# The order of the matmuls inside each product P times V, in a two-layer hybrid decoder trunk

## The chip, the cores and the metric

The kernel runs on one core of one Trainium2 chip. The metric is the device time of one execution in microseconds; less is better. A core has a matrix engine (TensorE: PE for its matmuls, PEld for its weight loads), a vector engine (DVE), a scalar engine (ACT), GpSimd (POOL), a queue engine (SP) and 16 DMA engines. Matmuls write their results to PSUM, eight banks of 512 fp32 values in each of 128 partitions; ACT and DVE carry them from there to the on-chip memory SBUF.

## The reference, cut to what matters

512 tokens of width 1024 pass two layers. Each layer is an attention part and a squared-ReLU MLP. What matters here are the attention products, which are all a softmax followed by a sum over keys:

```
# layer A, for each of 12 heads (3 groups of 4), two branches with the same form
p_s = masked_softmax(einsum('bgrqd,bgqkd->bgrqk', q_b, k_g) * scale, m_s)
o_s = einsum('bgrqk,bgqkd->bgrqd', p_s, v_g)            # selected blocks
p_w = masked_softmax(einsum('bgrqd,bgkd->bgrqk', q_b, k_b) * scale, m_w)
o_w = einsum('bgrqk,bgkd->bgrqd', p_w, v_b)             # sliding window
return g_b[..., 0:1] * o_c + g_b[..., 1:2] * o_s + g_b[..., 2:3] * o_w
...
# both layers, 4 heads over 256 memory tokens
p = softmax(einsum('bhqd,bhmd->bhqm', q, k) * scale)
o_mem = einsum('bhqm,bhmd->bhqd', p, v)
...
# layer B, 8 head slots, three dilated windows merged by their softmax sums
s = where(valid, einsum('bhqd,bhqkd->bhqk', q_b[:, gi], k_g) * scale, NEG)
outs.append(einsum('bhqk,bhqkd->bhqd', exp(s - lse), v_g))
```

With 512 tokens the window of 512 and the 16 selected blocks both cover every earlier token, so both branches of layer A are causal attention over different keys and values.

## The kernel before

**The order of things.** Layer A's attention comes first, then its MLP, then layer B's attention, then its MLP. Attention work is cut into items. An item has a front (scores, maximum, exponential, scaling) and a back (transposes of P, their evacuation, and, in the last item of a unit, the product P times V). `attend` (line 126) writes front k+1 before back k, and after each of them takes steps from a list of other work (projections, weight splits, output projection). The order in which the program writes instructions is not yet the order on the engine: line 1782 opens the framework's context with `schedule_with_timeline_sim=True`, which orders each engine's instructions by when they are ready on a simulated timeline, and among ready ones by the order of the program. What order came out is read from the trace. On the chip each engine then takes its list in that order.

**One unit of P times V.** V is the stationary operand, 128 keys by 64 columns; the transposed P is the moving one. Two heads share one PSUM bank, taken from the pool `pO` with a single buffer: the first head writes partitions 0 to 63, the second 64 to 127. So a matmul occupies 64 of the array's 128 columns, and the two heads' matmuls use different halves. A matmul on fp32 data is two instructions on PE. There are 24 units:

- **Layer A, `attn_a` lines 1023 to 1061.** For each of 3 groups, 2 pairs of heads (`pr`) and 2 halves of the queries (`half`, 256 queries each), items run over `hp` (which head of the pair) and `ii` (which 128 queries); the unit is written in the last of the four, hp = 1 and ii = 1. Half 0 has 2 blocks of 128 keys, half 1 has 4, in 2 branches `br`, for 2 heads: 8 and 16 matmuls, the last block of each branch over 128 columns, the others over 256. In half 0 both branches of an item are transposed into one bank and evacuated by one instruction; in half 1 each branch has its own (lines 1039 to 1043), branch 0 first. The transposed P lies in tiles of the tag `pt4`, four buffers. After half 1, `cmp_out` (line 955) adds one more matmul to the same bank and splits the sum for the output projection.
- **Memory attention, `mem_items` lines 600 to 620.** 2 pairs of heads in each layer. A head's P is transposed in 2 items (`ih`); the unit has 2 key blocks for 2 heads, 4 matmuls of 512 columns.
- **Layer B, `close0` line 1567 and `close1` line 1581,** one each for 4 pairs of slots. In `close0` 4 key blocks `j` for 2 slots `s`, 8 matmuls (256 columns, the last block 128); item ih = 0 of a slot brings the transposed columns 0 to 383, ih = 1 columns 384 to 895. In `close1` 4 residues `r` for 2 slots, 8 matmuls of 128 columns; ih = 0 brings r = 0 and 1, ih = 1 brings r = 2 and 3. A slot's items come before those of the next slot.

**Evacuation of transposes.** `evT` (line 656) copies a transposed bank to SBUF: in layer A every third time on DVE (line 658), otherwise on ACT (line 660); in layer B always on ACT. Transposes take banks from the pool `pT`, two buffers.

Of the kernel before, what the change touches and what calls it, by code (L numbers as in the profile page):

```python
# [18 lines left out]
NB = 4  # L19
# [145 lines left out]
class K:  # L165
# [412 lines left out]
    def mem_items(self, kf, qm, kk, outs, seg, need):  # L578

        nc = self.nc  # L580

        def front(h, ih):
            Sp = self.ps(self.pS, [P, 2, NMEM])
            for ii in range(2):
                i = ih * 2 + ii
                for hl in (0, 1):
                    nc.tensor.matmul(
                        Sp[:, ii, :], qm[0][h // 2][:, h % 2, i * P : (i + 1) * P], kk[0][hl][:, h, :],
                        start=hl == 0, stop=hl == 1,
                    )  # L590
            p, sm = self.soft(Sp, 2, NMEM)
            c = self.t("cr", [P, 2])
            nc.vector.reciprocal(out=c, in_=sm)
            for ii in range(2):
                self.pscale(p[:, ii, :], c[:, ii : ii + 1])
            return p

        pT = {}

        def back(h, ih, p):  # L600
            if ih == 0:
                pT[h] = self.t("pt4", [P, 2, S])
            pt = self.ps(self.pT, [P, 2, 2, P])
            for kb in range(2):
                for ii in range(2):
                    nc.tensor.transpose(pt[:, kb, ii, :], p[:, ii, kb * P : (kb + 1) * P], self.idf)
            self.evT(pT[h][:, :, ih * 256 : (ih + 1) * 256].rearrange("p k (i q) -> p k i q", q=P), pt)
            if h % 2 == 0 or ih == 0:
                return
            O = self.ps(self.pO, [P, S])  # L610
            for kb in range(2):
                for hp in range(2):
                    hh = h - 1 + hp
                    nc.tensor.matmul(
                        O[hp * 64 : hp * 64 + 64, :], kf[0][kb][1][:, hh * HD : (hh + 1) * HD], pT[hh][:, kb, :],
                        start=kb == 0, stop=kb == 1,
                    )
            oT = self.t("act", [P, 2, S], F32R)
            self.split(oT, O)
            outs.append(oT)  # L620

        return [Item(front, back, (h, ih), seg, need) for h in range(4) for ih in range(2)]

    def hilo(self, ki, src):
# [336 lines left out]
    def attn_a(self, g, ga, gt, cmp, out):  # L961


        nc = self.nc
        st, cs, Os = {}, [], []

        def cfront(i):
            if not cs:
                cs.extend(self.cmp_scores(g, ga[0], cmp, gt))
            return cs[2](i)  # L970

        def cback(i, s):
            cs[3](i, s)
            if i == NB - 1:
                cs.append(True)
                close()

        def close():
            while Os and len(cs) > 4:
                self.cmp_out(*Os.pop(0), *cs[0:2], out)  # L980

        def front(pr, half, hp, ii):
            q4, kk, v = ga
            h = pr * 2 + hp
            q = q4[pr][:, hp, :]
            i = half * 2 + ii
            n = (i + 1) * P
            blk = slice(i * P, (i + 1) * P)
            sm = self.t("su", [P, 2])
            if i <= 1:  # L990
                Sp = self.ps(self.pS, [P, 2, n])
                for hl in (0, 1):
                    nc.tensor.matmul(Sp, q[:, blk], kk[hl][:, :, 0:n], start=hl == 0, stop=False)
                nc.tensor.matmul(Sp[:, :, blk], self.idb, bcast(self.cm, 1, 2), start=False, stop=True)
                Sb = [Sp[:, 0, :], Sp[:, 1, :]]
                nm = self.t("nm", [P, 2])
                nc.vector.tensor_reduce(out=nm, in_=Sp, axis=AX.X, op=ALU.max, negate=True)
                nms = [nm[:, 0:1], nm[:, 1:2]]
                pp = self.t("p2", [P, 2, n])
                p = [pp[:, 0, :], pp[:, 1, :]]  # L1000
            else:
                Sb, nms = [], []
                for br in range(2):
                    Sp = self.ps(self.pS, [P, n])
                    for hl in (0, 1):
                        nc.tensor.matmul(Sp, q[:, blk], kk[hl][:, br, 0:n], start=hl == 0, stop=False)
                    nc.tensor.matmul(Sp[:, blk], self.idb, self.cm, start=False, stop=True)
                    nm = self.t("nm", [P, 1])
                    nc.vector.tensor_reduce(out=nm, in_=Sp, axis=AX.X, op=ALU.max, negate=True)
                    Sb.append(Sp)  # L1010
                    nms.append(nm)
                p = [self.t("p2", [P, n]) for _ in range(2)]
            o = (4 * g + h) * 3 + 1
            for br in range(2):
                nc.scalar.activation(p[br], Sb[br], AF.Exp, bias=nms[br], accum_out=sm[:, br : br + 1])
            c = self.t("cr", [P, 2])
            nc.vector.reciprocal(out=c, in_=sm)
            nc.vector.tensor_tensor(out=c, in0=c, in1=gt[:, i, o : o + 2], op=ALU.mult)  # L1018
            for br in range(2):
                self.pscale(p[br], c[:, br : br + 1])  # L1020
            return p

        def back(pr, half, hp, ii, p):
            v = ga[2]
            i = half * 2 + ii
            if ii == 0:
                if half == 0:
                    t = self.t("pt4", [P, 2, 2, 256])
                    st[hp] = [t[:, 0], t[:, 1], t]
                else:  # L1030
                    st[hp] = [self.t("pt4", [P, 4, 256]) for _ in range(2)]
            if i <= 1:
                pt = self.ps(self.pT, [P, 2, i + 1, P])
                for br in range(2):
                    for j in range(i + 1):
                        nc.tensor.transpose(pt[:, br, j, :], p[br][:, j * P : (j + 1) * P], self.idf)
                self.evT(st[hp][2][:, :, 0 : i + 1, ii * P : (ii + 1) * P], pt)
            else:
                for br in range(2):
                    pt = self.ps(self.pT, [P, i + 1, P])  # L1040
                    for j in range(i + 1):
                        nc.tensor.transpose(pt[:, j, :], p[br][:, j * P : (j + 1) * P], self.idf)
                    self.evT(st[hp][br][:, 0 : i + 1, ii * P : (ii + 1) * P], pt)
            if hp == 0 or ii == 0:
                return
            if half == 0:
                st["O"] = self.ps(self.pO, [P, S])
            O = st["O"]
            q0 = half * 256
            nj = 2 * half + 2  # L1050
            for br in range(2):
                for j in range(nj):
                    o = P if j == nj - 1 else 0
                    for x in range(2):
                        nc.tensor.matmul(  # L1055
                            O[x * 64 : x * 64 + 64, q0 + o : q0 + 256], v[:, j, br, :], st[x][br][:, j, o:256],
                            start=half == 0 and br == 0 and j == 0, stop=False,
                        )
            if half == 1:
                Os.append((O, pr))  # L1060
                close()

        order = [(pr, half, hp, ii) for pr in range(2) for half in range(2) for hp in range(2) for ii in range(2)]
        need = f"g{g}" if g else None
        return (
            [Item(front, back, a, g, need) for a in order],
            [Item(cfront, cback, (i,), g, "cmp") for i in range(NB)],
        )
# [409 lines left out]
    def attn_b(self, sp, q4, kv, oT, side):  # L1478
# [4 lines left out]
        t0, t1 = {}, {}  # L1483
# [83 lines left out]
        def close0():  # L1567
            vn = kv[1]
            O = self.ps(self.pO, [P, S])
            for j in (0, 2, 1, 3):  # L1570
                n = min(2, NB - j) * P
                for s in range(2):
                    nc.tensor.matmul(
                        O[s * 64 : s * 64 + 64, j * P : j * P + n], vn[:, j, s * HD : (s + 1) * HD],
                        t0[s][:, j * 256 : j * 256 + n], start=j == 0, stop=j == NB - 1,
                    )
            a = self.t("raw", [P, S])
            nc.scalar.activation(a.rearrange("p (r u) -> p r u", r=4), self.perm(O), AF.Copy)
# [2 lines left out]
        def close1():  # L1581
            vp = kv[2]
            O = self.ps(self.pO, [P, S])
            for r in range(4):
                for s in range(2):
                    nc.tensor.matmul(
                        O[s * 64 : s * 64 + 64, r * P : (r + 1) * P], vp[:, r, s * HD : (s + 1) * HD], t1[s][:, r, :],
                        start=True, stop=True,
# [198 lines left out]
```

## Time and profile before

| What | Value |
|---|---|
| time, median of 3 runs | 1309.15 us |
| the 3 runs | 1308.75 to 1311.78 us |
| the profiled execution, its own time | 1312.09 us |
| its span, first to last instruction | 1310.1 us |
| granted TensorE clock, mean over the span | 0.993 |
| DVE busy | 989.7 us (76%) |
| ACT busy | 766.2 us (58%) |
| POOL busy | 537.6 us (41%) |
| matmul instructions of P times V: line 1055 / 614 / 1573 / 1586 | 288 / 32 / 64 / 64 |

How to read it: an engine's busy time is the union of its instructions' times. The ends of matmuls are modelled and successive ones overlap a little, so the time that a group of matmuls really takes is best read from its start to the start of the next instruction on PE. A row of the timeline merges neighbours of one line: `213.25 1.73 PE L1055 ... x16` starts 213.25 us into the span, lasts 1.73 us and holds 16 instructions; a bracket at its end gives the engine's idle time before it and what ended that. The chain of waits is followed back from the last instruction, at each step to what released it. Layer A's attention lies between about 60 and 345 us of the span, layer B's between about 760 and 960 us.

### The profile page before, as it was taken

To read this page: it belongs to the slowest core of one execution; us is meant where nothing else is said; L and a number is where in the kernel's file an instruction comes from. 1 tells how busy PE (TensorE), PEld (TensorE's weight loads), DVE (VectorE), ACT (ScalarE), POOL (GpSimd) and SP (SyncE) were. 2 spreads that over 40 slices of the span, in tenths; PEclk is the share of its full clock that TensorE was granted. 3 is DMA by queue.
4 is the path that set the end of the run, shared out by engine and by line. 5 is a ranking of instruction groups with operands and counts; after the bars stand their busy time and mean duration, and the time that the engine had idled before them with its cause. 6 is when DMAs were issued, how large, how long until landed. Compare 5 with 4: busy or idle time off the path is not lost.

```text
span 1310.1 us, 18597 instructions
## 1 busy us (share of the span) xinstructions
PE 1267.1 (97%) x6425; PEld 1018.0 (78%) x6425; DVE 989.7 (76%) x1687; ACT 766.2 (58%) x1763; POOL 537.6 (41%) x569
## 2 busy tenths in 40 slices
PE   8998999999999999999999999999899999999998
PEld 6776677677787888888878898787578788788886
DVE  6878768764669678697799768776658968779678
ACT  5657657673465364554656477776756545355462
POOL 3756375542165142251333946441417424134241
PEclk9999999999999999999999999989999999999999
DMA  8313211023422525415244333012232442633423
GB/s 307 103 59 100 65 33 57 9 66 105 153 97 74 170 81 175 145 65 177 81 141 145 102 104 95 22 32 73 88 122 94 128 145 81 184 106 115 144 96 113
DMA packets 52686, 139.11 MB, mean 106 GB/s; under 512 B 5776, under 2 KB 14992, under 8 KB 52592
## 3 DMA queue, kind: packets, MB, share of 16 engines
q1 hardware_dynamic: 51376, 134.66, 32.4%
q0 software_dynamic: 640, 2.21, 0.5%
q8 instruction: 51, 0.84, 0.3%
q10 hardware_dynamic: 576, 1.05, 0.2%
q14 instruction: 43, 0.35, 0.1%
HBM read 132.66 MB, written 5.24 MB: 105 GB/s over the span
## 4 chain that ended last, share of the span: by engine, by line
PE 66%; DVE 21%; ACT 6%; DMA 3%; issue 2%; POOL 1%; SPq 0%; ACTq 0%; DVEq 0%; POOLq 0%
PE s_ps L238 10%; PE s_ps L239 10%; PE s_ps L237 10%; DVE s_w L232 7%; PE s_acc L237 4%; PE s_acc L238 4%; PE s_acc L239 4%; PE s_pt L238 3%; PE s_pt L239 3%; PE s_pt L237 3%; PE s_po L1055 2%; DVE s_p L1114 2%; DVE s_qk L275 2%; ACT s_w L230 2%; DVE s_w L254 1%
## 5 line engine op out<-in xcount | busy, mean ns | idle before, releaser
L232 DVE TENSOR_TENSOR s_w<-s_st,s_w 128x1024 fp32r<-128x1024 f32 (+4 forms) x155 | 182.9, 1182 | 133.7 <-ACT s_w L230 133.5
L230 ACT ACTIVATE s_w<-s_st 128x1024 fp32r<-128x1024 f32 (+4 forms) x182 | 166.2, 917 | 136.4 <-PE s_pt L239 35.4
L237 PE MATMUL s_ps<-s_act,s_w 128*128 128x512 f32 x592 | 231.8, 393 | 2.1 <-ACT s_act L272 1.4
L238 PE MATMUL s_ps<-s_act,s_w 128*128 128x512 f32 x592 | 231.1, 390 | 0.0
L239 PE MATMUL s_ps<-s_act,s_w 128*128 128x512 f32 x592 | 230.9, 391 | 0.0
L1100 POOL TENSOR_TENSOR s_x<-s_x,s_st 128x512 f32<-128x512 f32 x64 | 106.0, 1680 | 91.3 <-DVE s_w L232 91.3
L237 PEld LDWEIGHTS s_ps<-s_act,s_w 128*128 128x128 f32 x592 | 110.9, 188 | 26.9 <-ACT s_act L272 3.1
L238 PEld LDWEIGHTS s_ps<-s_act,s_w 128*128 128x128 f32 x592 | 111.2, 188 | 23.8 <-issue 0.8
L239 PEld LDWEIGHTS s_ps<-s_act,s_w 128*128 128x128 f32 x592 | 111.1, 188 | 23.5 <-issue 0.8
L237 PE MATMUL s_acc<-s_w,s_act 128*128 128x512 f32 (+2 forms) x304 | 111.5, 372 | 9.5 <-ACT s_w L230 6.0
L1100 POOL TENSOR_TENSOR s_x<-s_qki,s_st 128x512 f32<-128x512 f32 x16 | 25.9, 1617 | 217.2 <-DMA s_st<-in_w_db_dram 195.4
L238 PE MATMUL s_acc<-s_w,s_act 128*128 128x512 f32 (+2 forms) x304 | 110.5, 364 | 0.6 <-DVE s_w L254 0.5
L239 PE MATMUL s_acc<-s_w,s_act 128*128 128x512 f32 (+2 forms) x304 | 108.3, 360 | 0.0
L652 POOL TENSOR_SCALAR s_p<-s_p,s_cr 128x256 f32<-128x256 f32 (+3 forms) x128 | 68.9, 553 | 62.7 <-DVE s_cr L1018 21.6
L232 DVE TENSOR_TENSOR s_w<-s_x,s_w 128x512 fp32r<-128x512 f32 x96 | 90.3, 983 | 4.0 <-ACT s_w L230 4.0
L275 DVE TENSOR_TENSOR s_qk<-s_p,s_qk 128x256 fp32r<-128x256 f32 (+1 forms) x96 | 83.9, 886 | 2.8 <-ACT s_qk L272 1.6
L230 ACT ACTIVATE s_w<-s_x 128x512 fp32r<-128x512 f32 x96 | 56.8, 624 | 41.0 <-POOL s_x L1100 41.0
L232 POOL TENSOR_TENSOR s_w<-s_st,s_w 128x512 fp32r<-128x512 f32 (+4 forms) x27 | 38.1, 1413 | 94.7 <-ACT s_w L230 94.7
L272 ACT ACTIVATE s_qk<-s_p 128x256 fp32r<-128x256 f32 (+1 forms) x96 | 47.0, 489 | 46.5 <-DVE s_p L1228 44.2
L237 PEld LDWEIGHTS s_acc<-s_w,s_act 128*128 128x128 f32 x304 | 58.3, 193 | 16.8 <-ACT s_w L230 6.5
L238 PEld LDWEIGHTS s_acc<-s_w,s_act 128*128 128x128 f32 x304 | 58.6, 193 | 7.0 <-DVE s_w L254 1.1
L1222 ACT ACTIVATE s_p<-s_ps 128x512 f32<-128x512 f32 x64 | 37.8, 591 | 44.2 <-PE s_ps L239 41.9
(357 smaller groups left out, 3243.8 us busy)
## 6 DMA issues: line engine op xcount, KB each, us to landing
s_st<-in_w_db_dram SPq DMA_DIRECT2D x80, 512.0 KB, 3.6
s_st<-in_w_up_dram SPq DMA_DIRECT2D x64, 512.0 KB, 3.8
s_st<-in_w_bq_dram SPq DMA_DIRECT2D x16, 384.0 KB, 3.6
s_st<-in_w_ag_dram SPq DMA_DIRECT2D x11, 512.0 KB, 4.2
s_act<-in_w_c_dram SPq DMA_DIRECT2D x8, 512.0 KB, 4.8
s_st<-in_w_mem_dram SPq DMA_DIRECT2D x8, 512.0 KB, 3.5
s_st<-in_w_ao_dram SPq DMA_DIRECT2D x16, 256.0 KB, 2.6
s_tq<-in_w_db_dram SPq DMA_DIRECT2D x16, 256.0 KB, 3.0
```

Source lines behind the costliest of these rows:

```text
L230: nc.scalar.activation(w[:, 0], st, AF.Copy)
L232: self.low = e.tensor_tensor(out=w[:, 1], in0=st, in1=w[:, 0], op=ALU.subtract)
L237: mm(ps, lh[0], rh[0], start=start, stop=False, skip_group_check=again)
L238: mm(ps, lh[0], rh[1], start=False, stop=False, skip_group_check=again)
L239: mm(ps, lh[1], rh[0], start=False, stop=stop, skip_group_check=again)
L272: nc.scalar.activation(dst[:, 0], src, AF.Copy)
L275: nc.vector.tensor_tensor(out=dst[:, 1], in0=src, in1=dst[:, 0], op=ALU.subtract)
L652: self.nc.gpsimd.tensor_scalar(out=p, in0=p, scalar1=c, scalar2=1.0, op0=ALU.mult, op1=ALU.mult)
L1055: nc.tensor.matmul(O[x * 64 : x * 64 + 64, q0 + o : q0 + 256], v[:, j, br, :], st[x][br][:, j, o:256], start=half == 0 and br == 0 and j = ...
L1100: self.nc.gpsimd.tensor_tensor(out=o, in0=x, in1=b[:, i * 512 : (i + 1) * 512], op=ALU.add)
L1114: tt = lambda o, x, y, op: nc.vector.tensor_tensor(out=o, in0=x, in1=y, op=op)
L1222: nc.scalar.activation(u, ps, AF.Relu)
```

## The change

In all five loops over matmuls the order is turned, so that the matmul written first is one whose moving operand is evacuated last: the second head before the first (`hp`, `x`, `s`), the second branch before the first (`br`), and in layer B the later key blocks first (`j`, `r`). The flag `start`, which makes the first write to a place overwrite what stands in the bank, goes with the first matmul. The matmuls are the same ones, with the same operands and sizes; only their order in the program differs. Transposes, evacuations, the other matmuls and all transfers are written as before.

```diff
@@ mem_items.back
             for kb in range(2):
-                for hp in range(2):
+                for hp in (1, 0):
                     hh = h - 1 + hp
@@ attn_a.back
-            for br in range(2):
+            for br in (1, 0):
                 for j in range(nj):
                     o = P if j == nj - 1 else 0
-                    for x in range(2):
+                    for x in (1, 0):
                         nc.tensor.matmul(
                             O[x * 64 : x * 64 + 64, q0 + o : q0 + 256], v[:, j, br, :], st[x][br][:, j, o:256],
-                            start=half == 0 and br == 0 and j == 0, stop=False,
+                            start=half == 0 and br == 1 and j == 0, stop=False,
                         )
@@ attn_b.close0
-            for j in (0, 2, 1, 3):
+            for j in (2, 0, 1, 3):
                 n = min(2, NB - j) * P
-                for s in range(2):
+                for s in (1, 0):
                     nc.tensor.matmul(
                         O[s * 64 : s * 64 + 64, j * P : j * P + n], vn[:, j, s * HD : (s + 1) * HD],
-                        t0[s][:, j * 256 : j * 256 + n], start=j == 0, stop=j == NB - 1,
+                        t0[s][:, j * 256 : j * 256 + n], start=j == 2, stop=j == NB - 1,
                     )
@@ attn_b.close1
-            for r in range(4):
-                for s in range(2):
+            for r in (2, 3, 0, 1):
+                for s in (1, 0):
                     nc.tensor.matmul(
```

## The prediction

> **What bounds the kernel now.** I read the page first, then the busy time by stretches, then the timeline of PE around every product P times V, then the chain of waits there.
>
> ```profile
> span 1310.1 us, 18597 instructions
> PE 1267.1 (97%) x6425; PEld 1018.0 (78%) x6425; DVE 989.7 (76%) x1687; ACT 766.2 (58%) x1763; POOL 537.6 (41%) x569
> PE 66%; DVE 21%; ACT 6%; DMA 3%; issue 2%; POOL 1%; SPq 0%; ACTq 0%; DVEq 0%; POOLq 0%
> ```
>
> PE is busy for 97% of the span and makes 66% of the chain. The stretches tell where it has room (columns: length, then busy time and number of instructions of PE, PEld, DVE, ACT, POOL, then granted clock, DMA share, GB/s):
>
> ```profile
> 60.00:103.00 43.00, 43.00 (x226) 33.09 (x225) 31.63 (x71) 25.55 (x79) 26.11 (x46) 1.00 0.25 86
> 103.00:155.00 52.00, 45.61 (x269) 32.38 (x267) 41.52 (x116) 38.31 (x115) 27.35 (x38) 0.93 0.33 103
> 155.00:200.00 45.00, 45.00 (x276) 35.75 (x274) 29.57 (x81) 25.12 (x74) 29.92 (x40) 1.00 0.09 26
> 200.00:250.00 50.00, 46.42 (x322) 33.10 (x320) 39.85 (x120) 36.69 (x116) 23.42 (x41) 1.00 0.11 37
> 250.00:305.00 55.00, 52.97 (x335) 39.92 (x336) 34.20 (x87) 39.33 (x120) 24.67 (x41) 1.00 0.20 59
> 305.00:345.00 40.00, 39.31 (x180) 27.80 (x179) 18.95 (x29) 12.38 (x26) 9.49 (x10) 1.00 0.37 113
> 800.00:940.00 140.00, 128.78 (x866) 104.30 (x865) 103.14 (x229) 101.03 (x328) 54.48 (x71) 0.98 0.21 62
> 940.00:960.00 20.00, 19.19 (x88) 11.50 (x87) 8.15 (x18) 12.00 (x32) 8.28 (x15) 1.00 0.03 9
> ```
>
> PE never rests in 60 to 103 and 155 to 200, and rests 0.7 us in 305 to 345 and 0.8 in 940 to 960: there its time is the time. It rests 6.4 us in 103 to 155, 3.6 in 200 to 250, 2.0 in 250 to 305 and 11.2 in 800 to 940: there a saving on PE can partly become waiting. The MLPs hold no changed line.
>
> **What the change moves: half 0 of layer A.** The timeline of PE, group 0, first pair:
>
> ```profile
> 77.91 0.65 PE L1055 MATMUL s_po<-s_pt,s_x 128*64 128x256 f32 x2
> 78.49 0.50 PE L237 MATMUL s_acc<-s_w,s_act 128*128 128x512 f32 x1
> 84.59 1.51 PE L1055 MATMUL s_po<-s_pt,s_x 128*64 128x256 f32 x14
> ```
>
> The unit's 16 instructions (8 matmuls) run in two pieces. The first head's first matmul is ready early and runs alone, 6.7 us ahead; the other seven come when the second head is transposed. Alone it takes 0.58 us from its start to the next (0.65 less 0.07 of overlap), while seven together take 1.51 less 0.07 = 1.44: the two heads fill different column halves and run side by side. The x14 piece holds all four matmuls of the second head and three of the first, so the fourth fits beside them, and 16 instructions together should again take 1.44. Each such unit saves **0.58**; there are six.
>
> **Half 1.** Group 1, first pair, with the two evacuations that it needs:
>
> ```profile
> 207.41 0.65 PE L1055 MATMUL s_po<-s_pt,s_x 128*64 128x256 f32 x2
> 212.46 0.59 ACT L660 ACTIVATE s_pt<-s_pt 128x512 f32<-128x512 f32 x1
> 213.25 1.73 PE L1055 MATMUL s_po<-s_pt,s_x 128*64 128x256 f32 x16
> 214.82 0.68 DVE L658 COPY s_pt<-s_pt 128x512 f32<-128x512 f32 x1
> 214.91 0.54 PE L677 MATMUL s_pt<-idr,s_qki 128*128 128x128 f32 x4
> 216.45 1.73 PE L1055 MATMUL s_po<-s_pt,s_x 128*64 128x256 f32 x14
> 218.10 1.12 PE L956 MATMUL s_po<-s_x,s_ki 128*128 128x512 f32 x2
> ```
>
> ```profile
> 164.39 3.24 PE L1055 MATMUL s_po<-s_pt,s_x 128*64 128x256 f32 x30
> ```
>
> 213.25 + 1.73 is 214.98 and the next starts at 214.91: the 0.07 above. Three pieces take 0.58 + 1.66 + 1.66 = 3.90. In group 0's second pair (the last row) 30 of the 32 instructions ran together, with all of the second head's, in 3.17. So 32 together should take 3.17, and a unit saves 0.73 (five of them) or 0.58 (that one). But the first piece of 16 ran here while branch 1 was still being evacuated, and now waits too. After the change PE does at 213.25 what stood between the pieces (214.91 to 216.45, 1.54 us), rests until the evacuation ends at 214.82 + 0.68 = 215.50, and needs 3.17 from there: done at 218.67 instead of 218.10, 0.57 later, just what the lone piece gives back. Net **0**. Where the two evacuations follow each other closely it is different:
>
> ```profile
> 259.81 0.62 ACT L660 ACTIVATE s_pt<-s_pt 128x512 f32<-128x512 f32 x1
> 260.19 1.73 PE L1055 MATMUL s_po<-s_pt,s_x 128*64 128x256 f32 x16
> 261.86 0.54 PE L677 MATMUL s_pt<-idr,s_qki 128*128 128x128 f32 x4
> 262.32 1.73 PE L1055 MATMUL s_po<-s_pt,s_x 128*64 128x256 f32 x14
> ```
>
> Here the last evacuation ends at 260.43. The 0.46 of line 677 fills the time until 260.65, and 3.17 more is 263.82, against 262.32 + 1.66 = 263.98: with the lone piece gone, **0.74** saved. Six units between 0 and 0.74: I take the middle, 2.2 in all.
>
> **Memory attention.**
>
> ```profile
> 313.54 1.07 PE L614 MATMUL s_po<-s_pt,s_act 128*64 128x512 f32 x2
> 318.65 1.93 PE L614 MATMUL s_po<-s_pt,s_act 128*64 128x512 f32 x6
> ```
>
> One of the four matmuls runs alone in 1.00; the other three take 1.86, as the second head's two set it. Together they should take 1.86: **1.00** saved, four times.
>
> **Layer B.** `close0` comes in three pieces, `close1` in three (rows of the second and of the third pair of slots):
>
> ```profile
> 830.49 0.65 PE L1573 MATMUL s_po<-s_pt,s_x 128*64 128x256 f32 x2
> 835.79 0.65 PE L1573 MATMUL s_po<-s_pt,s_x 128*64 128x256 f32 x4
> 835.89 0.60 ACT L660 ACTIVATE s_pt<-s_pt 128x512 f32<-128x512 f32 x1 [0.75 <-PE s_pt L1551]
> 836.37 0.53 PE L677 MATMUL s_pt<-idr,s_qki 128*128 128x128 f32 x4
> 836.83 1.30 PE L1573 MATMUL s_po<-s_pt,s_x 128*64 128x256 f32 x10
> ...
> 886.12 0.43 PE L1586 MATMUL s_po<-s_pt,s_x 128*64 128x128 f32 x2
> 888.74 0.66 PE L1586 MATMUL s_po<-s_pt,s_x 128*64 128x128 f32 x8
> 906.84 0.65 PE L1586 MATMUL s_po<-s_pt,s_x 128*64 128x128 f32 x6
> ```
>
> `close0`: 0.58 + 0.58 + 1.23 = 2.39 now. Its 16 instructions have per head three matmuls of 256 and one of 128 columns, like the x16 row at 213.25, so 1.66: 0.73 less. The last evacuation ends at 836.49; before it PE has only the 0.46 of line 677; done at 836.49 + 1.66 = 838.15 against 838.06. With the lone 0.58 gone, **0.49** remains. `close1`: 0.36 + 0.59 + 0.58 = 1.53 now. One matmul a head costs 0.36 and two cost 0.59, so four cost about 0.59 + 2 x 0.23 = 1.05: 0.48 less. But after the last evacuation 1.05 follows instead of 0.58, 0.47 later, against the 0.59 of the x8 piece: **0.12** where that piece counts.
>
> **What of it lies on the path.** If every piece counted, PE would have 6 x 0.58 + 5 x 0.73 + 0.58 + 4 x 1.00 + 4 x 0.73 + 4 x 0.48 = 16.6 us less to do. The chain of waits says which lone pieces count:
>
> ```profile
> 313.62 1.00 PE s_po L614 x2
> ```
>
> Such a row stands in the chain for 4 of the 6 lone pieces of half 0, for 5 of 6 of half 1, for all 4 of the memory units and for 3 of 4 of `close0`; for `close1` it is the x8 piece in 3 of 4. The rest lie beside a DMA, DVE or ACT that the chain follows, and I cost them at nothing. The sum is 4 x 0.58 = 2.3, 2.2 for half 1, 4.0, 3 x 0.49 = 1.5 and 3 x 0.12 = 0.4: 10.4. Of this, about 4 lie in 103 to 155, 200 to 250 and 800 to 940 (two half-0 units, three half-1 units, layer B), where PE already rests 21 us in all; I let half of it go into new rests, 2.1. That leaves **8.3 us**. From the profiled execution's 1312.09 it gives 1303.8; it lies 2.9 above the median of the runs, and I take the difference over: 1309.15 - 8.3 = **1300.9**.
>
> **What else is moved.** No DMA and no evacuation is added. Each unit's first matmul now waits for the last evacuation, and everything behind it in PE's list waits with it; who needs that are the next scores and transposes, and through them DVE and ACT. The `pO` bank is taken later and freed when it was; nobody else asks for it in between. In half 1 the four `pt4` buffers of a unit were freed from the x16 piece on; now the first come free halfway through the 3.17 block, up to 3 us later, and the next pair's evacuation needs one. At 213.25 the next transposes ran only after line 956 at 218.10, so I cost this at nothing; its cover is the other work of PE, and without it the price is in the first rival.
>
> The neighbours of a piece:
>
> ```profile
> 79.28 0.38 PE L1036 MATMUL s_pt<-c,s_p 128*128 128x128 f32 x2
> 79.41 0.47 PE L239 MATMUL s_acc<-s_w,s_act 128*128 128x512 f32 x1
> 79.73 0.39 PE L237 MATMUL s_acc<-s_w,s_act 128*128 128x512 f32 x1
> ```
>
> A projection matmul lasts 0.39 behind its like (79.73), 0.50 behind a lone piece (78.49) and 0.47 behind transposes (79.41). Since most pieces stand between transposes and such matmuls, I count 0.03, that is nothing, for the place that a piece leaves. [...]
>
> **The rivals.**
>
> *Slower: the early pieces were free.* They filled PE while it waited for evacuations, and now each whole unit runs after the last one. Then nothing is saved, and what follows the last evacuation grows by 3.17 - 1.66 = 1.51 in five half-1 units, 1.66 - 1.23 = 0.43 in four `close0`, 0.47 in four `close1`: 7.6 + 1.7 + 1.9 = 11.2 us, 1320. It decides where PE has less other ready work than the evacuation lasts, as at 213.25. Added rests can also lower the clock: the granted 0.93 in 103 to 155 took 0.07 x 52 = 3.6 us, and half as much again would be 1.8 more. Against this rival: the pieces stand in the chain, and 60 to 103, 155 to 200 and 305 to 345 have no rest to fill. 0.12.
>
> *No difference: the time turns into waits.* DVE is busy 41.5 of 52 and 39.9 of 50 us where PE rests, so in those stretches the next softmax sets the pace; only the memory units and a little else pay, and the half-1 delays eat the rest: 2 us, 1307. It also holds the case that the new order does not join the pieces. 0.18.
>
> *All of it counts:* 16.6 us, 1292.5, if later scores move ahead of the postponed products and DVE starts sooner. 0.08.
>
> **How the numbers follow.** The forecast, 4 to 15 us less, has 0.62. A change within 0.3%, about 3.9 us, cannot be told from none. Faster is 0.62 + 0.08 = 0.70, the same 0.18, slower 0.12. The range leaves out the first and the last rival: 1294 to 1311, from 15 us less to just above today.
>
> **What would show it.** Right: no row of two instructions of line 1055, 614, 1573 or 1586 by itself; units as single rows of about 1.5, 3.2, 1.9, 1.7 and 1.1 us; 305 to 345 shorter by 2 us, 940 to 960 too; slightly more rest on PE before these rows, ended by lines 658 and 660. Wrong: rests of more than 1 us before the half-1 rows, a lower granted clock in 200 to 305, units that still come in pieces, or joined units that last as long as their pieces did.

## The result, and the profile after

The changed kernel takes 1302.7 us (median of 7 runs, 1299.5 to 1303.6) against 1309.15 us (7 runs beside it, 1308.2 to 1317.4): a ratio of 0.9932 with a 95% interval of 0.9908 to 0.9955, so 6 to 12 us less (the ratio lies near that of the means; the two medians alone give 0.9951). Forecast were 1300.9 us, 8.3 less. The profiled execution took 1302.66 us against 1312.09 us.

The page of after: span, busy times by engine, and the shares of the chain of waits.

```profile
span 1300.6 us, 18592 instructions
PE 1252.5 (96%) x6425; PEld 1017.7 (78%) x6425; DVE 987.0 (76%) x1687; ACT 765.6 (59%) x1763; POOL 540.1 (42%) x569
PE 59%; DVE 24%; ACT 10%; DMA 3%; issue 2%; POOL 2%; ACTq 0%; POOLq 0%; DVEq 0%
```

PE has 14.6 us less to do, the span is 9.5 us shorter: 5.1 us became rest. The chain shows the same: PE's share falls from 66% to 59%, DVE and ACT rise from 27% to 34%. The other engines' busy times hardly move.

Now the units in the timeline of PE in after, one of each kind (for half 1 with the last evacuation and its neighbours):

```profile
84.88 1.52 PE L1055 MATMUL s_po<-s_pt,s_x 128*64 128x256 f32 x16
132.73 3.25 PE L1055 MATMUL s_po<-s_pt,s_x 128*64 128x256 f32 x32 [0.94 <-ACT s_pt L660]
...
204.98 0.67 DVE L658 COPY s_pt<-s_pt 128x512 f32<-128x512 f32 x1
207.71 0.37 PE L239 MATMUL s_acc<-s_w,s_act 128*128 128x256 f32 x1
208.00 3.25 PE L1055 MATMUL s_po<-s_pt,s_x 128*64 128x256 f32 x32
211.18 1.12 PE L956 MATMUL s_po<-s_x,s_ki 128*128 128x512 f32 x2
...
311.12 1.94 PE L614 MATMUL s_po<-s_pt,s_act 128*64 128x512 f32 x8
820.84 1.09 PE L1586 MATMUL s_po<-s_pt,s_x 128*64 128x128 f32 x16 [0.31 <-ACT s_pt L660]
829.30 1.73 PE L1573 MATMUL s_po<-s_pt,s_x 128*64 128x256 f32 x16 [0.39 <-ACT s_pt L660]
```

All 24 units run in one piece. Less the overlap of 0.07 they take 1.45, 3.18, 1.87, 1.02 and 1.66 us, in the order of the rows; the forecast had 1.44, 3.17, 1.86, 1.05 and 1.66. The longest rest in front of a half-1 unit is the 0.94 at 132.73, and the unit at 208.00 has none: its last evacuation ended at 205.65, but PE still had projections (line 239) to do.

Three landmarks in the timeline show where the time went: the first transposes of each MLP (line 1144) and the first scores of layer B (line 1501). Before, then after:

```profile
342.38 0.38 PE L1144 MATMUL s_pt<-c,s_x 128*128 128x128 f32 x2
768.87 0.22 PE L1501 MATMUL s_ps<-s_qk,s_qk 128*128 128x128 f32 x1
960.06 0.38 PE L1144 MATMUL s_pt<-c,s_x 128*128 128x128 f32 x2
```

```profile
333.48 0.38 PE L1144 MATMUL s_pt<-c,s_x 128*128 128x128 f32 x2
759.77 0.22 PE L1501 MATMUL s_ps<-s_qk,s_qk 128*128 128x128 f32 x1
951.69 0.38 PE L1144 MATMUL s_pt<-c,s_x 128*128 128x128 f32 x2
```

At the first landmark after is 8.90 us ahead, at the second 9.10, at the third 8.37, and at the end 9.5. So layer A's attention gave nearly everything, and layer B's attention **nothing** (0.7 us longer), although two of the four memory units lie in that stage too. The busy times of the two stages (columns as in the prediction's second fence), before, then after:

```profile
60.00:342.38 282.38, 269.69 (x1582) 199.88 (x1580) 193.11 (x496) 177.26 (x525) 140.81 (x212) 0.99 0.22 68
768.87:960.06 191.19, 179.17 (x1161) 145.01 (x1161) 137.33 (x293) 136.10 (x437) 84.52 (x110) 0.98 0.20 59
```

```profile
60.00:333.48 273.48, 259.49 (x1585) 197.18 (x1584) 193.86 (x497) 176.52 (x525) 144.91 (x213) 0.99 0.22 70
759.77:951.69 191.92, 175.23 (x1161) 147.25 (x1161) 137.11 (x293) 136.52 (x437) 83.41 (x110) 0.96 0.20 58
```

In layer A PE lost 10.2 us of work and gained only 1.3 of rest. In layer B its busy time fell by 3.9 us, but its rest grew from 12.0 to 16.7, and the granted clock in the stage fell from 0.98 to 0.96. A lower clock makes the same work last longer (in after a projection matmul of line 239 lasts 0.63 us at 921.25, in a stretch at half clock, and 0.39 at 916.70), so 3.9 is less than what the new order took off PE. The experiments ask which part gives what, and why layer B gives nothing.

### The profile page after: what moved, and what is told of

It reads as the page before. It is cut to its first block, busy times and chain, and to the rows that moved or that the text cites. A ratio compares the mean times of both kernels' runs of the same rounds, so it can differ in the third digit from the quotient of the medians.

```text
span 1300.6 us, 18592 instructions
## 1 busy us (share of the span) xinstructions
PE 1252.5 (96%) x6425; PEld 1017.7 (78%) x6425; DVE 987.0 (76%) x1687; ACT 765.6 (59%) x1763; POOL 540.1 (42%) x569
## 3 DMA queue, kind: packets, MB, share of 16 engines
q10 hardware_dynamic: 576, 1.05, 0.2%
## 4 chain that ended last, share of the span: by engine, by line
PE 59%; DVE 24%; ACT 10%; DMA 3%; issue 2%; POOL 2%; ACTq 0%; POOLq 0%; DVEq 0%
PE s_ps L238 10%; PE s_ps L239 10%; PE s_ps L237 10%; DVE s_w L232 7%; PE s_acc L237 4%; PE s_acc L238 4%; PE s_acc L239 4%; DVE s_p L1114 2%; PE s_po L1055 2%; PE s_pt L238 2%; PE s_pt L239 2%; PE s_pt L237 2%; ACT s_w L230 2%; DVE s_w L254 2%; DVE s_qk L275 2%
```

## The experiments

All edits are against the kernel before, unless said otherwise. "Clock" is the granted TensorE clock over the span, as a mean over the runs; the runs of before beside them had 0.9952 (e1 to e4), 0.9943 (e5 to e8) and 0.9941 (e9 to e12), and medians of 1309.8, 1311.4 and 1311.2 us.

| Run | What it holds | us | Ratio to before, 95% | Clock |
|---|---|---|---|---|
| e1 | layer A's units | 1304.2 | 0.9955 (0.9941 to 0.9969) | 0.9948 |
| e2 | memory units | 1305.8 | 0.9969 (0.9957 to 0.9980) | 0.9953 |
| e3 | layer B's units | 1311.6 | 1.0011 (0.9998 to 1.0024) | 0.9914 |
| e4 | all, but head after head | 1323.4 | 1.0098 (1.0081 to 1.0114) | 0.9906 |
| e5 | layer A and memory | 1300.0 | 0.9918 (0.9904 to 0.9931) | 0.9952 |
| e6 | all units, heads only | 1304.3 | 0.9949 (0.9936 to 0.9961) | 0.9896 |
| e7 | layer B, heads only | 1312.5 | 1.0007 (0.9993 to 1.0021) | 0.9922 |
| e8 | layer A's half 0 | 1309.2 | 0.9984 (0.9975 to 0.9993) | 0.9938 |
| e9 | the full change again | 1300.9 | 0.9924 (0.9904 to 0.9943) | 0.9915 |
| e10 | full, early matmuls added | 1302.6 | 0.9933 (0.9916 to 0.9950) | 0.9915 |
| e11 | e5, without the turn of branches | 1301.2 | 0.9918 (0.9900 to 0.9936) | 0.9952 |
| e12 | e5 and `close0` | 1301.7 | 0.9924 (0.9907 to 0.9940) | 0.9925 |

### The three parts by themselves: e1, e2, e3

e1, in `attn_a`:

```diff
-            for br in range(2):
+            for br in (1, 0):
...
-                    for x in range(2):
+                    for x in (1, 0):
...
-                            start=half == 0 and br == 0 and j == 0, stop=False,
+                            start=half == 0 and br == 1 and j == 0, stop=False,
```

> Only the loops over br and x in layer A are turned; memory units and layer B stand as before. Theory P (a lone piece wastes half of the array; joining the pieces takes that time off PE): the 12 units last 1.45 and 3.18 us, end of the second memory unit about 5 to 7 us earlier than before (the full change has 8.9 there, of which 2 belong to the memory units), time 1302 to 1305. Rival S (the gain is a matter of what other work the new order lets go first, and the units' own time does not matter): no tie to the number of units, anything from 1298 to 1312.

e2, in `mem_items`:

```diff
-                for hp in range(2):
+                for hp in (1, 0):
```

> Only the loop over hp in the memory units is turned. Theory P: four units of 1.87 instead of 1.00 + 1.86; 2 us off each layer's attention, 4 in all, or 2 if layer B gives its share back: 1305 to 1307. Rival S: 1309 within 0.2%.

e3, in `close0` and `close1`:

```diff
-            for j in (0, 2, 1, 3):
+            for j in (2, 0, 1, 3):
...
-                for s in range(2):
+                for s in (1, 0):
...
-                        t0[s][:, j * 256 : j * 256 + n], start=j == 0, stop=j == NB - 1,
+                        t0[s][:, j * 256 : j * 256 + n], start=j == 2, stop=j == NB - 1,
...
-            for r in range(4):
-                for s in range(2):
+            for r in (2, 3, 0, 1):
+                for s in (1, 0):
```

> Only close0 and close1 are turned. In the full change layer B's attention gave back 0.7 us of what layer A had gained, where 1.9 us of further gain were forecast, and it shows 17.1 us at half clock against 6.8 before. Theory C (the added rests before the joined units let the clock drop there): units of 1.67 and 1.02, yet layer B no shorter than before, with 10 us or more at half clock between 760 and 960, time 1307 to 1311. Rival W (the joined units come too late and all else waits, at any clock): as long or longer with no more than 7 us at half clock.

Layer A's units give 0.0045 x 1309.8 = 5.9 us (4.1 to 7.7), the memory units 4.1 (2.6 to 5.6), layer B's units -1.4 (-3.1 to 0.3). The product of the three ratios is 0.9935; the full change has 0.9932 and 0.9924 (e9). Within the intervals the parts add up. Layer B's stage in the windows of e3, between the same two landmarks:

```profile
767.22:960.76 193.54, 177.62 (x1161) 148.32 (x1161) 137.16 (x293) 136.55 (x437) 83.68 (x110) 0.95 0.20 58
```

PE is busy for 1.6 us less there than before and yet the stage is 2.4 us longer, at a clock of 0.95 instead of 0.98: 20.5 us at half clock, as theory C expected.

### Do the two heads have to alternate: e4

The full change, with its loops exchanged, so that all matmuls of the second head are written before those of the first:

```diff
-            for kb in range(2):
-                for hp in (1, 0):
+            for hp in (1, 0):
+                for kb in range(2):
...
-            for br in (1, 0):
-                for j in range(nj):
-                    for x in (1, 0):
+            for x in (1, 0):
+                for br in (1, 0):
+                    for j in range(nj):
...
-            for j in (2, 0, 1, 3):
-                for s in (1, 0):
+            for s in (1, 0):
+                for j in (2, 0, 1, 3):
...
-            for r in (2, 3, 0, 1):
-                for s in (1, 0):
+            for s in (1, 0):
+                for r in (2, 3, 0, 1):
```

> The full change, but within each unit all of the second head's matmuls come before the first head's, so that the halves of the array hardly work side by side; the first matmul still needs the last evacuation and the pieces are joined. Theory P: units of about 2.7, 6.1, 3.6, 3.1 and 1.9 us instead of 1.45, 3.18, 1.87, 1.67 and 1.02; 6 x 1.25 + 6 x 2.95 + 4 x 1.7 + 4 x 1.45 + 4 x 0.87 = 41 us more on PE than the full change, 30 to 41 of them in the time: 1333 to 1344. Rival S: the joining alone does it, 1300 to 1306.

The units in the timeline of PE in e4 (half 0, half 1, memory, `close1`, `close0`):

```profile
84.29 2.22 PE L1055 MATMUL s_po<-s_pt,s_x 128*64 128x256 f32 x16
211.92 5.67 PE L1055 MATMUL s_po<-s_pt,s_x 128*64 128x256 f32 x32
327.02 1.94 PE L614 MATMUL s_po<-s_pt,s_act 128*64 128x512 f32 x8
837.98 1.58 PE L1586 MATMUL s_po<-s_pt,s_x 128*64 128x128 f32 x16 [0.31 <-ACT s_pt L660]
846.80 2.65 PE L1573 MATMUL s_po<-s_pt,s_x 128*64 128x256 f32 x16 [0.39 <-ACT s_pt L660]
```

They are one piece each, as in after, but longer by 0.70, 2.42, 0, 0.49 and 0.92 us. So it is the pairing of the heads that makes a unit short: the theory that a unit takes as long as its matmuls run in pairs holds, the rival that only the count of pieces matters falls. In all PE has 6 x 0.70 + 6 x 2.42 + 4 x 0.49 + 4 x 0.92 = 24.4 us more work than in the full change, and the time is 1.0098 / 0.9932 = 1.67% or 21.8 us longer: **0.9 us of time for 1 us of PE** (the two intervals leave room for 0.7 to 1.1). The expected 1333 to 1344 was missed: the extra was too large because I had counted no pairs at all. The memory unit, four matmuls written head after head, takes the same 1.87 us as in alternation; the half-0 unit loses just the pairs at its two ends. Both lengths come out if the first head's first matmul starts beside the one two places ahead of it in the list. The starts of the single instructions in the trace bear this out for all five kinds: in the half-1 unit, for one, the second head's first six matmuls start one by one, and the first start beside another comes 2.43 us into the unit, 0.01 behind the start of the second head's seventh of eight matmuls.

### Which part of the turn does it: e6, e11, e8, e5

e6 turns only the heads, everywhere (`hp`, `x` and both `s`), and leaves branches, blocks and `start` as before:

```diff
-                for hp in range(2):
+                for hp in (1, 0):
...
-                    for x in range(2):
+                    for x in (1, 0):
...
-                for s in range(2):
+                for s in (1, 0):
```

> Only the order of the heads is turned (hp, x, s); branches and key blocks run in the old order. Each piece then holds whole pairs: 8 + 8 matmuls in half 1, 2 + 6 in close0, 4 + 4 in close1, one piece in half 0 and in the memory units. Theory P with C: PE does 6 x 0.15 + 4 x 0.14 + 4 x 0.16 = 2.1 us more than in the full change, but the early pieces fill rests and keep the clock: 1297 to 1301, clock 0.993 or more. Rival T (it is the first matmul's waiting for what is transposed last that brings the gain): half 1 and layer B lose theirs, 1304 to 1307.

Its third half-1 unit and a `close0` in the timeline of PE:

```profile
207.21 1.73 PE L1055 MATMUL s_po<-s_pt,s_x 128*64 128x256 f32 x16
210.40 1.73 PE L1055 MATMUL s_po<-s_pt,s_x 128*64 128x256 f32 x16
...
827.97 0.65 PE L1573 MATMUL s_po<-s_pt,s_x 128*64 128x256 f32 x4
829.02 1.30 PE L1573 MATMUL s_po<-s_pt,s_x 128*64 128x256 f32 x12
```

A half-1 unit comes here in two pieces of whole pairs, 1.66 us each, 3.32 against 3.18 in one piece; the first does not wait for branch 1. No matmul runs alone. I had expected that the early pieces keep PE busy and the clock up; that fell, the clock is 0.9896, the lowest of all. The time, 1304.3, missed the expected 1297 to 1301 too and lies where rival T had put it, so e6 by itself speaks for T. To be free of layer B, e11 leaves that out and turns the heads in `attn_a` and `mem_items` alone:

```diff
-                for hp in range(2):
+                for hp in (1, 0):
...
-                    for x in range(2):
+                    for x in (1, 0):
```

> Layer A with only the heads turned (branches in the old order, so that half 1 runs as 8 + 8 whole pairs), the memory units turned, layer B as before. Theory P: as e5, 1298 to 1301 (PE 0.9 us more in half 1, but its first piece no longer waits for the second branch), clock 0.994 or more. Rival T (waiting for what is transposed last matters): 1303 or more.

e5 is e1 and e2 together, so the full change without layer B:

```diff
+            for br in (1, 0):
+                    for x in (1, 0):
+                            start=half == 0 and br == 1 and j == 0, stop=False,
...
+                for hp in (1, 0):
```

> The full change without layer B's close0 and close1, which stand as before. Theory P with C (every joined unit takes time off PE, but in layer B the rests before the joined units lower the clock and eat it): the parts add, 0.9955 x 0.9969 = 0.9924 of before, about 1299.9, with a mean clock of 0.994 or more; no slower than the full change and perhaps 1 to 2 us faster. Rival W (nothing to do with the clock, layer B's part is worth its 1.9 us): slower than the full change, 1304.

e5 and e11 have the same ratio, 0.9918: **in layer A turning the branches adds nothing that can be told**; the order of the heads does it, and rival T, which had 1303 or more for e11, falls there. What made e6 slow is then layer B's share: e11's and e7's ratios multiply to 0.9925, and e6's 0.9949 is 3 us more, about as much as the three intervals leave room for. What gains is that no matmul of one head runs without a partner. That the whole unit waits for the last transposed tile is not needed for it.

e8 turns the heads and branches nowhere but for `x` in half 0:

```diff
-                    for x in range(2):
+                    for x in (0, 1) if half else (1, 0):
```

> Layer A's half 0 alone: the second head first. Forecast: four of six lone pieces count, 2.3 us, 1307.5. If all six count, 3.5 us, 1306.3. The rest of layer A's 5.9 us belongs to half 1, forecast at 2.2.

0.0016 x 1311.4 = 2.1 us (0.9 to 3.3) for six lone pieces. Half 1 is then, by difference, 0.9955 / 0.9984 = 0.9971, 3.8 us, with an interval of some 2.2 either way.

### Why layer B gives nothing: e7, e10, e12, e9

First theory: the joined units leave rests while PE waits for the last evacuation, and the clock falls for that. e7 turns only the heads in layer B, so that pieces of whole pairs still run early:

```diff
-                for s in range(2):
+                for s in (1, 0):
```

> Layer B's close0 and close1 alone, and of them only the order of the slots s: pieces of 2 + 6 and 4 + 4 matmuls. Theory C: early pairs run before the last evacuation as before the change, so the rests and the clock stay as before (0.995); 1.81 instead of 2.39 and 1.18 instead of 1.53 us, 3.7 us less on PE, of which 1.5 to 3 in the time: 1307 to 1308.5. Rival W: as with the whole of layer B's change, 1310 to 1312.

In this form it fell: 1312.5 us, a ratio of 1.0007 and a clock of 0.9922, close to what rival W expected. As in e6, pieces of whole pairs run early, and neither time nor clock is better than in e3. The old rests are not back in e7, though: between the landmarks PE rests 15.2 us in e7's stage, against 12.0 before. So the run clears the wait of the joined units, but not rest as such.

Second theory: the early lone matmuls, useless as they were, kept the clock up. e10 is the full change with such a matmul put back in front of each `close0` and `close1`; it is extra work, and its result is overwritten:

```diff
+            nc.tensor.matmul(O[0:64, 256:512], vn[:, 0, 0:HD], t0[0][:, 0:256], start=True, stop=True)
             for j in (2, 0, 1, 3):
...
+            nc.tensor.matmul(O[0:64, 256:384], vp[:, 0, 0:HD], t1[0][:, 0, :], start=True, stop=True)
             for r in (2, 3, 0, 1):
```

> The full change, and in close0 and close1 the lone first matmul is put back as an extra one whose result the unit then overwrites (256 and 128 columns, first slot, ready early). PE does 4 x 0.58 + 4 x 0.36 = 3.8 us more than in the full change. Theory C2 (layer B is paced by other engines, so PE time taken off it becomes rest, and with more rest the clock drops; the lone pieces filled it): mean clock back to 0.993 or more and the time equal to the full change or up to 3 us less. Rival K (the clock in layer B drops for the joined units' place, whatever else runs): clock 0.990, time 0 to 4 us more than the full change.

e9 is the full change once more, to stand beside it:

> The full change once more, beside the next three on the same chip, because the clock differs between runs: 0.9932 of before again, mean clock 0.990, against 0.994 to 0.996 for the kernels that leave layer B alone.

The profiled execution of e9 had a clock of 0.994 and so shows the full change without the drop. Layer B's stage, between the landmarks:

```profile
761.03:949.70 188.67, 171.18 (x1161) 143.29 (x1161) 136.31 (x293) 136.20 (x437) 83.90 (x110) 0.98 0.21 60
```

At the clock of before, 0.98, the stage is 2.5 us shorter than before: PE is busy for 8.0 us less, and 5.5 of them became rest. Of the 2.5, some 2.0 belong to the two memory units in the stage, if they give what they were forecast to. The same kernel's profile in after, with 10.2 us more at half clock, has a stage 3.3 us longer. So one profile's clock is not the kernel's, and even at the old clock nearly all of what `close0` and `close1` save becomes rest.

A `close0` in the timeline of PE in e10, and layer B's stage in its windows:

```profile
824.44 0.65 PE L1570 MATMUL s_po<-s_pt,s_x 128*64 128x256 f32 x2
829.43 1.74 PE L1574 MATMUL s_po<-s_pt,s_x 128*64 128x256 f32 x16 [0.39 <-ACT s_pt L660]
```

```profile
759.25:951.96 192.71, 179.60 (x1178) 148.58 (x1178) 138.31 (x293) 136.32 (x437) 82.78 (x110) 0.96 0.20 58
```

The lone matmul runs early, 5 us ahead, and the clock is 0.9915, just that of e9. This theory fell too: PE's busy time in the stage is back to that of before (179.60 against 179.17) and its rest nearly so (13.1 against 12.0), and the clock is not. The time is 0.09% above e9's; the intervals leave room for nothing as well as for all of the added 3.8 us.

e12 adds `close0` alone to e5:

```diff
-            for j in (0, 2, 1, 3):
+            for j in (2, 0, 1, 3):
...
-                for s in range(2):
+                for s in (1, 0):
...
-                        t0[s][:, j * 256 : j * 256 + n], start=j == 0, stop=j == NB - 1,
+                        t0[s][:, j * 256 : j * 256 + n], start=j == 2, stop=j == NB - 1,
```

> e5 and close0 of layer B; close1 as before. Forecast of the prediction for close0: 1.5 us less than e5, 1298.5. Theory C2: 0 to 3 us more than e5 with a clock below 0.993, because close0 takes 0.73 x 4 = 2.9 us off PE in a stage that PE does not pace.

0.9924 against e5's 0.9918 cannot be told apart, but the clock can: 0.9925 against 0.9952. The time, 1301.7 against 1300.0, is within what theory C2 expected and not the 1.5 us less of the prediction. Layer B's stage in the windows of e5, then of e12:

```profile
760.23:951.48 191.25, 178.66 (x1161) 145.78 (x1161) 136.39 (x293) 136.40 (x437) 84.90 (x110) 0.97 0.21 59
```

```profile
760.34:950.84 190.50, 174.39 (x1161) 144.54 (x1161) 137.28 (x293) 135.93 (x437) 83.79 (x110) 0.97 0.20 59
```

With `close0` turned PE is busy for 4.3 us less there (4 x 0.73 = 2.9 were forecast), at the same clock in these two profiles; 3.5 of the 4.3 became rest, and the stage is 0.75 shorter. Two single profiles do not give the exact sizes: e11, with layer B as in e5, has 176.15 us of busy PE between the landmarks, at a clock of 0.99. Seven kernels turn something in `close0` (the full change, e3, e4, e6, e7, e10, e12), and all of them run at a mean clock of 0.9896 to 0.9925; the kernels without one have 0.9938 to 0.9953. What that costs can be read from runs of one kernel: in the 12 runs of e3 the two at a clock of 0.988 took 1314.3 and 1316.2 us, the two at 0.995 took 1309.1 and 1310.7, about 0.8 us for 0.001. 0.003 less is then some 2.5 us, more than the 1.9 that were forecast for layer B's units. At a clock of 0.995 e3's 1309.1 and 1310.7 stand beside 1310.3, the mean of the five runs of before at that clock that were made beside them: even without the loss hardly anything would be gained, as in e9's profile.

**Open:** why the clock is lower when `close0` is turned (with `close1` in all of these kernels but e12; no run turns `close1` alone). It is not the wait of the joined units alone (e7) and not the missing lone matmuls (e10). More rest of PE remains the likeliest reason and is not shown: between the landmarks PE rests 13.1 to 17.5 us in the profiles of the kernels that turn `close0` and 11.8 to 13.3 in the others, but e9 rests most and kept its clock in that execution, and no run has the saved PE time without the rests.

## Why the prediction was right

The total was right, and so was the mechanism in layer A and the memory units: the lone matmuls went, the units became single rows, as long as forecast. That the total came out as close as it did is in part luck, since layer A gave more than was forecast and layer B nothing. By the prediction's steps:

- **Lengths of joined units:** right within 0.03 us for all five kinds.
- **Half 0, 2.3 us:** measured 2.1 (0.9 to 3.3). Right.
- **Memory units, 4.0 us:** measured 4.1 (2.6 to 5.6). Right.
- **Half 1, 2.2 us:** 3.8 by difference, with an interval that reaches down to 1.6. If wrong, too small, and the step would be "done at 218.67 instead of 218.10, 0.57 later". I left PE's list as it was and let PE rest until the evacuation. In after the list behind the unit is another one: at 208.00 projections stood ahead of it, and there was no rest.
- **Layer B, 1.9 us before the discount:** wrong, -1.4 (-3.1 to 0.3): the 1.9 is excluded, a gain of nothing is not. The PE time was saved, but turned into rests, and the clock fell. The prediction had named the lower clock as a danger for stretches of layer A only, 103 to 155 and 200 to 305, and had put it in the slower rival with half of 3.6 us.
- **The discount of 2.1 us for new rests:** spread over both layers it was wrong in both. Layer A and memory together gave 10.7 us (9.0 to 12.6, e5), where 11.7 would be all of their PE time and 8.5 less about 1 were forecast. Layer B gave nothing. In the sum one error stands against the other: 8.3 forecast, 6.4 by the two medians, 8.9 by the ratio, 10.0 in e9.
- **Taking over the 2.9 us** by which the profiled execution lay above the median: fair; the profiled executions differ by 9.4 us and the medians by 6.4 and 10.3.

The rivals: "the early pieces were free" fell for layer A, where the rests before half-1 units were at most 0.94 us. "The time turns into waits" is what layer B did, but not the DVE-bound stretches of layer A, as far as these windows of after tell:

```profile
103.00:155.00 52.00, 46.84 (x294) 35.54 (x293) 45.49 (x133) 40.99 (x123) 32.38 (x46) 0.97 0.32 103
195.00:245.00 50.00, 45.12 (x335) 32.99 (x333) 37.29 (x119) 36.42 (x118) 25.69 (x44) 1.00 0.11 37
245.00:300.00 55.00, 52.45 (x337) 40.32 (x333) 35.12 (x86) 38.53 (x120) 25.97 (x41) 0.97 0.22 68
```

More instructions of PE fit in the first two of them than before (294 against 269, 335 against 322): that fits stretches which became shorter as well, although PE has rests there, but the windows do not hold the same work. One sign that was to show the prediction wrong is there, a clock of 0.97 in 245 to 300 where it was 1.00; but 103 to 155 rose from 0.93, and layer A's mean is 0.99 in both kernels. "All of it counts" is close for layer A and memory, 10.7 of 11.7.

The place that a lone piece leaves was counted as nothing: a projection matmul of before lasts 0.50 us behind one (78.49), 0.47 behind transposes (79.41) and 0.39 behind its like (79.73). If each of the 21 pieces that go in layer A and the memory units gave back the whole 0.50 - 0.39 = 0.11, an estimate from these rows, 2.3 us more and 14.0 in all would be on offer there, of which 10.7 came. No run tells which of the two it was, 11.7 or 14.0.

## What to carry to other kernels

When two small matmuls share the array, begin the list with the operand that comes last, and alternate: a matmul that runs ahead without its partner costs as much as the pair would (0.65 us alone at 830.49 in before, 0.65 for the pair at 827.97 in e6), and joining 24 units was 0.7% here. In layer A and the memory units 1 us taken off PE was 0.9 us of time (e5), and 1 us added over all units was 0.9 too (e4), even where the chain of waits names other engines now and then; in layer B's units it was nothing. PE's busy share would not have told the two apart: it was 95.5% in layer A's stage and 93.7% in layer B's, where two of the memory units lie too, and the 2.6 us that the memory units gave at the least is more than two of them can. What a saving is worth was told only by trying each part by itself, with the granted clock read over many runs. Here layer B's edits can be left out, and in layer A and the memory units the heads' order alone does what the whole change does.

## What the hardware showed that was not expected

**The clock falls in steps of about 3.4 us, in a stage where PE is busy more than 90% of the time** (layer B's in after, 175.23 of 191.92 us). Two stretches of after in the windows, and the second of them cut where the clock steps:

```profile
846.00:852.00 6.00, 5.42 (x36) 5.34 (x35) 5.56 (x13) 3.87 (x13) 4.96 (x6) 0.72 0.28 80
918.00:930.00 12.00, 10.64 (x44) 8.07 (x43) 6.38 (x14) 8.44 (x26) 3.33 (x6) 0.57 0.34 101
915.71:919.12 3.41, 1.94 (x10) 1.12 (x9) 2.36 (x5) 1.45 (x4) 0.45 (x1) 1.00 0.59 150
919.12:929.36 10.24, 9.86 (x40) 7.52 (x40) 5.67 (x12) 7.00 (x23) 2.56 (x5) 0.50 0.30 93
```

The last two rows have a clock of 1.00 and of 0.50. If it is one or the other throughout, the mean of 0.72 over 6 us is 3.4 us at half clock, and 0.57 over 12 us is 10.3, three times as much. The traces of before and after show more. Between 25 and 1290 us every stretch at half clock in them lasts 3.41 us, or two or three times that, and the starts lie whole multiples of 3.413 us apart, to 0.01 (in after at 116.99, 277.41, 407.12, 806.48, 847.44 and 919.12: 47, 38, 117, 12 and 21 times). Cut both traces into windows of 3.413 us, counted from the first fall: the clock fell ten times, each time after a window in which PE was busy for 0.87 to 2.71 of the 3.41 us, as the profile counts busy (before: 1.73, 2.71, 2.02 and 0.87; after: 2.08, 1.75, 2.17, 1.79, 1.47 and 1.94). At full clock, all of the 5 windows with at most 1.79 us were followed by half clock, none of the 688 with more than 2.72 was, and 5 of the 33 between these were; 840.61 to 844.03 in after, with 1.93, was not. One of the ten windows has a single rest of 1.66 us in it (after, 275.14 to 276.80). What rest it takes is not shown. Where the windows fall differs from execution to execution: the first fall is at 129.24 in before and at 116.99 in after, 3.6 windows apart.

**Matmuls of two column halves overlap beyond their order in the list.** In e4 the memory unit's four matmuls, head after head, still take 1.87 us and not 4 x 0.93 = 3.7 (two of one head take 1.86, before, 318.65). So they did not start in the order of the list: the third matmul must have run beside the first, before the second had started. In the trace the unit's first two instructions start 0.01 us apart (e4, 327.02), while those of a lone matmul start 0.48 apart (before, 313.54). This takes the list to have the program's order within a unit, as it had in before, where one matmul of the first head ran ahead and the head's others, ready too, did not.
